# The output projection's sum over the heads by ScalarE and an accumulating DMA

## The chip, the cores and the metric

The kernel runs on one core of one Trainium2 chip. The metric is the device time of one execution in microseconds (us), as the median of several executions. Engines: TensorE (PE), VectorE (DVE), ScalarE (ACT), GpSimd (POOL), and SyncE (SP), which issues the transfers of the kernel before.

## The reference, cut to what matters

Two layers: a Hyena long convolution, then differential attention with 16 heads. 512 positions and 16 meta tokens, width 1024, inner width 2048, all float32. The change lies in the last line of the second layer, the product with `w_out`:

```python
def diff_attention_mixer(h, w_in, lam_vecs, subln, w_out, cos, sin, layer_idx):
    u = h @ w_in                                  # q, k, v, z
    ...
    o = rmsnorm(o, subln, DA_NORM_EPS) * (1.0 - lam_init)      # per head, 128 wide
    return (o.reshape(B, T, D_INNER) * jax.nn.silu(z)) @ w_out
# reference: h = h + rmsnorm(y, norm_post[i]); return h[:, N_META:]
```

The kernel sums this product over the heads: each head gives 128 of the 2048 rows of `w_out`, and `acc` (in SBUF, 4 blocks of 128 positions by 1024 columns) holds the sum.

## The kernel before, in words

Each float32 matmul is made of three products of rounded parts (`hi`, L209, on ACT; `lo`, L212, the rest, on DVE or POOL). The attention stage runs from 855 us to the end. `attend` (L1282) takes one head per step: for four blocks of 128 queries it does `scores` (L1302: matmuls L1315 and L1318 into two `a` tiles of PSUM, maximum L1321 on DVE, exponentials L1322 on ACT into `pp` and `E`, their difference L1326 on DVE, a copy of 80 columns L1327 on POOL), and for the head before it `turn` (L1330: transposes into a `b` tile, casts to `ph`, `pl`) and `weigh` (L1347: the product with the values). Between these, `run` lets a `Filler` put in steps from a list `seq`, by a credit in us: projections of queries and keys of the next head, in odd steps the `z` projections of two heads (L345 into a `b` tile, L1231 on DVE empties it, L1233 is its tanh), in even steps the values of two heads, and the output projection of the head two before. A scheduler then orders the instructions of each engine; the order is fixed in the program. The four `b` tiles ("b", one PSUM bank each) are taken in turn by projections, transposes and products, so that each matmul into a `b` tile waits until the instruction that emptied the same bank four tiles before is done.

The output projection is `o_item` (L1236): for each block `tt` of 128 positions, six matmuls L1249 into two banks, one per half of the 1024 columns. How the banks get into the sum depends on the head. Head 0: ACT writes them (L1262). Heads 1 to 12: DVE multiplies by the row's factor `r` and adds to `acc` (L1264, 128x512, two per block). Head 13: ACT moves both banks to `vl` (L1254) and POOL adds (L1255). Heads 14 and 15: DVE, both banks in one instruction (L1257). Head h's projection stands in step h + 2, so that of head 13 lies beside the last head's weighted sums, in the tail, from some 1387 us on. After the last head, `finish` (L1059 on) applies the norm and writes the output.

The tile `E` also holds the lambda vectors once, ahead of the heads (L1001). `vl` holds the low parts of the values (rows 0 to 3 are used; L1211 puts the fifth row's low part into `vh`).

Of the kernel before, what the change touches and what calls it, by code (L numbers as in the profile page):

```python
# [10 lines left out]
F32 = mybir.dt.float32  # L11
F32R = mybir.dt.float32r
I32 = mybir.dt.int32
AF = mybir.ActivationFunctionType
ALU = mybir.AluOpType
# [4 lines left out]
P = 128  # L20
T = 528
TH = 264
PARTS = ((0, 272, 68), (272, 528, 128))
META = 16
S = 512
D = 1024
E = 2048
KT = 8
NCH = 8
HEADS = 16  # L30
MR = 6 * META
# [102 lines left out]
def view(t, off, *dims, parts=None):  # L134
    pd = list(t.ap[0])
    if parts is not None:
        pd = [pd[0], parts]
    return bass.AP(tensor=t.tensor, offset=t.offset + off, ap=[pd] + [list(x) for x in dims])
# [54 lines left out]
class Trunk:  # L193
# [777 lines left out]
    def attention(self):  # L971
        tc, nc, I = self.tc, self.nc, self.I
        v, g, s, te = nc.vector, nc.gpsimd, nc.scalar, nc.tensor
        with ExitStack() as cx:
            pool = lambda name, **kw: cx.enter_context(tc.tile_pool(name=name, **kw))
            k1 = pool("k1", bufs=1)
            pc = pool("pc", bufs=2)
# [20 lines left out]
            self.load(sub, I["subln"])  # L998
            v.tensor_scalar(sub, sub, 0.5 * (1.0 - LAM_INIT), None, op0=ALU.mult)

            lv = self.tl(pc, [P, 4, 64], F32, "E", bufs=2)  # L1001
            self.load(lv, bass.AP(tensor=I["lam"].tensor, offset=0, ap=[[0, P], [64, 4], [1, 64]]))
            v.tensor_tensor(lv[:, 0::2], lv[:, 0::2], lv[:, 1::2], op=ALU.mult)
            l2 = self.tl(k1, [P, 2], F32, "l2")
# [178 lines left out]
    def v_item(self, pc, u, st):  # L1183

        def body(wv, j):
            te = self.nc.tensor
            if j == 0:
                st["vh"] = self.tl(pc, [P, 5, 256], F32R, "vh", bufs=2)
                st["vl"] = self.tl(pc, [P, 5, 256], F32R, "vl", bufs=2)
            a, b = KTS[j]  # L1190
            n = P if j < 4 else MR
            ps = self.tl(self.psB, [P, 512], F32, "b")
            for k in range(KT):
                wk = slice((k % 4) * 256, (k % 4) * 256 + 256)
                if j < 4:
                    ops = [(self.xh[:, k, a:b], 0), (self.xh[:, k, a:b], 1), (self.xl[:, k, a:b], 0)]
                else:
                    xm = self.xm[:, k].rearrange("p a b c -> p (a b c)")
                    ops = [(xm, 0), (xm, 1)]
                for q, (x, w) in enumerate(ops):  # L1200
                    te.matmul(ps[:n, :256], x, wv[k // 4][w][:, wk], start=(k == 0 and q == 0),  # L1201
                              stop=(k == KT - 1 and q == len(ops) - 1))
            r = self.rv[:n, j:j + 1]
            vh = st["vh"][:n, j]
            self.nc.scalar.activation(vh, ps[:n, :256], AF.Copy, scale=r)
            if j < 4:
                o, lo = slice(0, n), st["vl"][:n, j]
            else:
                o = slice(64, n)
                lo = st["vh"][o, j]  # L1210
            self.nc.vector.scalar_tensor_tensor(lo, ps[o, :256], r[o], vh[o].bitcast(F32), op0=ALU.mult,  # L1211
                                                op1=ALU.subtract)

        return Item([self.I["w_v"][u, i] for i in (0, 1)], [(2.6 if j < 4 else 1.75, lambda w, j=j: body(w, j)) for j in range(5)])

    def z_item(self, pc, st):
# [19 lines left out]
    def o_item(self, pc, st, then=None):  # L1236

        def body(ws, tt):
            (gh, gl), (wh, wl) = st["g"], ws[0]
            r = st["r"][:, tt:tt + 1]  # L1240
            if st["h"] < HEADS - 3:
                pss = [self.tl(self.psB, [P, 512], F32, "b") for _ in (0, 1)]
            else:
                both = self.tl(self.psA, [P, 2, 512], F32, "a")
                pss = [both[:, 0], both[:, 1]]
            sls = [slice(0, 512), slice(512, D)]
            for q, (a, b) in enumerate(((gh, wh), (gh, wl), (gl, wh))):
                for ps, sl in zip(pss, sls):
                    self.nc.tensor.matmul(ps, a[:, tt * P:(tt + 1) * P], b[:, sl], start=q == 0, stop=q == 2)  # L1249
            if st["h"] >= HEADS - 3:  # L1250
                y = self.yo[:, tt].rearrange("p (h n) -> p h n", h=2)
                if st["h"] == HEADS - 3:
                    t = self.tl(pc, [P, 2, 512], F32, "vl", bufs=2)
                    self.nc.scalar.activation(t, both, AF.Copy, scale=r)  # L1254
                    self.nc.gpsimd.tensor_tensor(y, y, t, op=ALU.add)  # L1255
                else:
                    self.nc.vector.scalar_tensor_tensor(y, both, r, y, op0=ALU.mult, op1=ALU.add)  # L1257
                pss = ()
            for ps, sl in zip(pss, sls):
                y = self.yo[:, tt, sl]  # L1260
                if st["h"] == 0:
                    self.nc.scalar.activation(y, ps, AF.Copy, scale=r)  # L1262
                else:
                    self.nc.vector.scalar_tensor_tensor(y, ps, r, y, op0=ALU.mult, op1=ALU.add)  # L1264
            if then:
                then(tt)

        return Item([self.I["w_out1"][st["h"]]], [(1.3, lambda w, tt=tt: body(w, tt)) for tt in range(4)])

    def attend_last(self, pc, st, sub, fill):  # L1270
# [31 lines left out]
    def scores(self, pc, st, qt, nlam):  # L1302

        v, s, te = self.nc.vector, self.nc.scalar, self.nc.tensor
        r2 = lambda t: t.rearrange("p (h t) -> p h t", h=2)
        s0, pr = st["s0"], st["pr"]
        ks, qs, ql = st["ks"], st["qs"], st["ql"]
        p = self.tl(pc, [P, MR + S], F32, "pp", bufs=8)
        es = [p[:, MR - META:], self.tl(pc, [P, T], F32, "E", bufs=2)]
        sm = self.tl(self.small, [P, 4], F32, "sm")  # L1310
        tq = slice(qt * P, (qt + 1) * P)
        pss = [self.tl(self.psA, [P, 2, 512], F32, "a") for _ in (0, 1)]
        for mp in (0, 1):
            for h in (0, 1):
                te.matmul(pss[mp][:, h, :TH], qs[:, mp, tq], ks[:, mp, h * TH:(h + 1) * TH], start=True, stop=False)  # L1315
        for mp in (0, 1):
            for h in (0, 1):
                te.matmul(pss[mp][:, h, :TH], ql[:, mp, tq], ks[:, mp, h * TH:(h + 1) * TH], start=False, stop=True)  # L1318
        for mp, ps in enumerate(pss):
            mx = self.tl(self.small, [P, 1], F32, "mx")  # L1320
            v.tensor_reduce(mx, ps[:, :, :TH], axis=AX.XY, op=ALU.max, negate=True)  # L1321
            s.activation(r2(es[mp]), ps[:, :, :TH], AF.Exp, bias=mx,  # L1322
                         accum_out=s0[:, qt:qt + 1] if mp == 0 else sm[:, 0:1])
        v.reciprocal(sm[:, 1:2], sm[:, 0:1])
        v.scalar_tensor_tensor(sm[:, 2:3], s0[:, qt:qt + 1], nlam, sm[:, 1:2], op0=ALU.mult, op1=ALU.mult)
        v.scalar_tensor_tensor(es[0], es[1], sm[:, 2:3], es[0], op0=ALU.mult, op1=ALU.add)  # L1326
        self.nc.gpsimd.tensor_copy(view(p, 0, [META, 5], [1, META]), view(p, MR - META, [0, 5], [1, META]))  # L1327
        pr.append(p)
# [79 lines left out]
```

## Time and profile before

| | us |
|---|---|
| median of 3 executions | 1432.77 (1430.24 to 1435.04) |
| the profiled execution, its own time | 1434.51 |
| its span, first to last instruction | 1432.4 |
| PE busy in the span | 1342.4 (94%) |
| DVE busy | 1138.2 (79%) |
| ACT busy | 735.2 (51%) |
| POOL busy | 519.1 (36%) |
| mean granted clock of PE, share of full | 0.972 |

The rows of the profile that follow come from this one execution. "Busy" counts time in which an engine works on an instruction; a matmul of 512 columns starts some 0.23 us after the one before it and ends later, since matmuls overlap. A wait is put down to the instruction that released it last. A DMA's time is that from its issue to its landing.

### The profile page before, as it was taken

The page shows a single profiled execution, that of the slowest core. Times are in us where ns is not written, and L with a number is a line of the kernel's source. Part 1 is how long each engine was busy: PE and PEld are TensorE (multiplying, and loading weights), DVE is VectorE, ACT ScalarE, POOL GpSimd, SP SyncE. Part 2 cuts the span into 40 slices and gives each one's busy share as a digit, 9 for nine tenths or more (in the row PEclk, how much of TensorE's full clock was granted, in tenths as well). Part 3 has the DMA queues.
Part 4 walks back from the last instruction along what each step waited for, and adds up shares of the span by engine and source line. Part 5 has one row for each costly group of instructions (what it writes and reads, how often), then busy time and mean ns, then how long its engine had stood idle before and what let it go on. Part 6 is the DMA issues. An engine that isn't in the chain of part 4 may idle for free. (4 is left out here: it accounts for less than half of the span.)

```text
span 1432.4 us, 24736 instructions
## 1 busy us (share of the span) xinstructions
PE 1342.4 (94%) x9296; PEld 1246.3 (87%) x9296; DVE 1138.2 (79%) x2196; ACT 735.2 (51%) x1400; POOL 519.1 (36%) x543
## 2 busy tenths in 40 slices
PE   5889999999999999999887999999999999999994
PEld 4889889999999999999887888897979879797883
DVE  8789988877777777777678687978879687888888
ACT  5355533443333232324447678666567556667653
POOL 7367634532323232323534233223342323324223
PEclk8899999999999999999988999999999999999998
DMA  6343442232323232323310312212021221212221
GB/s 207 103 146 124 145 153 75 74 119 75 104 74 104 75 103 75 103 74 101 95 62 32 132 45 75 70 42 81 31 88 60 67 67 38 82 45 89 89 67 59
DMA packets 63558, 123.47 MB, mean 86 GB/s; under 512 B 7296, under 2 KB 11648, under 8 KB 63440
## 3 DMA queue, kind: packets, MB, share of 16 engines
q1 hardware_dynamic: 63440, 121.91, 26.2%
q8 instruction: 73, 1.20, 0.3%
q14 instruction: 45, 0.37, 0.1%
HBM read 109.30 MB, written 12.58 MB: 85 GB/s over the span
## 5 line engine op out<-in xcount | busy, mean ns | idle before, releaser
L209 ACT CAST wh<-wr 128x512 fp32r<-128x512 f32 x314 | 182.1, 618 | 253.3 <-PE b L348 70.4
L348 PE MATMUL b<-xh,wh 128*128 128x264 f32 x1024 | 264.9, 291 | 3.8 <-ACT wh L209 1.9
L348 PE MATMUL b<-xl,wh 128*128 128x264 f32 x1024 | 263.5, 289 | 2.6 <-DVE xl L458 2.6
L348 PE MATMUL b<-xh,wl 128*128 128x264 f32 x1024 | 258.5, 288 | 0.6 <-POOL wl L212 0.6
L212 DVE TENSOR_TENSOR wl<-wr,wh 128x512 fp32r<-128x512 f32 x250 | 182.7, 760 | 25.3 <-ACT wh L209 24.1
L348 PEld LDWEIGHTS b<-xh,wh 128*128 128x128 f32 x1024 | 184.0, 193 | 7.6 <-ACT wh L209 2.7
L348 PEld LDWEIGHTS b<-xl,wh 128*128 128x128 f32 x1024 | 183.8, 192 | 4.3 <-DVE xl L458 3.9
L348 PEld LDWEIGHTS b<-xh,wl 128*128 128x128 f32 x1024 | 181.7, 192 | 1.1 <-POOL wl L212 0.9
L212 POOL TENSOR_TENSOR wl<-wr,wh 128x512 fp32r<-128x512 f32 x64 | 97.4, 1538 | 83.8 <-ACT wh L209 83.7
L345 PE MATMUL b<-xh,wh 128*128 128x512 f32 x232 | 94.3, 406 | 4.8 <-DVE acc L1264 4.8
L1321 DVE TENSOR_REDUCE mx<-a 128x1 f32<-128x528 f32 x128 | 87.9, 700 | 7.7 <-PE a L1318 7.2
L345 PE MATMUL b<-xl,wh 128*128 128x512 f32 x232 | 93.6, 403 | 0.0
L345 PE MATMUL b<-xh,wl 128*128 128x512 f32 x232 | 93.0, 401 | 0.0
L1264 DVE SCALAR_TENSOR_TENSOR acc<-b,rh,acc 128x512 f32<-128x512 f32 x96 | 70.8, 743 | 25.9 <-PE b L1249 25.3
L1179 POOL TENSOR_TENSOR ro<-ro,rope 128x528 f32<-128x528 f32 (+1 forms) x32 | 43.1, 1347 | 108.6 <-ACT ro L1168 102.1
L514 POOL TENSOR_SCALAR u<-vecs 128x1 f32<-128x1 f32 x96 | 26.4, 296 | 151.7 <-DVE cv L519 133.5
L1327 POOL COPY pp<-pp 128x80 f32<-128x80 f32 x64 | 16.5, 259 | 166.6 <-DVE pp L1326 120.0
L1201 PE MATMUL b<-wh,xh 128*128 128x256 f32 x256 | 73.9, 289 | 0.4 <-DVE vl L1211 0.4
L1201 PE MATMUL b<-wl,xh 128*128 128x256 f32 x256 | 72.8, 284 | 0.0
L1201 PE MATMUL b<-wh,xl 128*128 128x256 f32 x256 | 72.5, 283 | 0.0
L1315 PE MATMUL a<-ks,qs 128*128 128x264 f32 x256 | 56.2, 302 | 10.0 <-ACT qs L209 6.2
L1315 PEld LDWEIGHTS a<-ks,qs 128*128 128x128 f32 x256 | 46.0, 194 | 21.4 <-ACT qs L209 6.4
(383 smaller groups left out, 4036.7 us busy)
## 6 DMA issues: line engine op xcount, KB each, us to landing
wr<-in_w_in SPq DMA_DIRECT2D x128, 256.0 KB, 2.9
wr<-in_w_out SPq DMA_DIRECT2D x64, 256.0 KB, 2.8
hsp<-ho SPq DMA_DIRECT2D x16, 512.0 KB, 2.7
H<-hsp SPq DMA_DIRECT2D x16, 512.0 KB, 3.9
wr<-in_w_k SPq DMA_DIRECT2D x32, 256.0 KB, 2.8
wr<-in_w_q SPq DMA_DIRECT2D x32, 256.0 KB, 2.7
wr<-in_w_z SPq DMA_DIRECT2D x32, 256.0 KB, 2.7
wr<-in_w_v SPq DMA_DIRECT2D x32, 256.0 KB, 2.6
```

Source lines behind the costliest of these rows:

```text
L209: self.nc.scalar.copy(dst, src)
L212: (eng or self.nc.vector).tensor_tensor(dst, src, hi.bitcast(F32), op=ALU.subtract)
L345: te.matmul(ps, w[:, wk], x[:, k, first:T], start=st, stop=sp)
L348: te.matmul(ps[h], w[:, wk], x[:, k, h * TH:(h + 1) * TH], start=st, stop=sp)
L514: g.tensor_scalar(u[:, e:e + 1], b_in[:, mt:mt + 1], -1.0, None, op0=ALU.mult)
L1179: g.tensor_tensor(y, y, rope[:, 1, n0:n0 + n], op=ALU.mult)
L1201: te.matmul(ps[:n, :256], x, wv[k // 4][w][:, wk], start=(k == 0 and q == 0), stop=(k == KT - 1 and q == len(ops) - 1))
L1264: self.nc.vector.scalar_tensor_tensor(y, ps, r, y, op0=ALU.mult, op1=ALU.add)
L1315: te.matmul(pss[mp][:, h, :TH], qs[:, mp, tq], ks[:, mp, h * TH:(h + 1) * TH], start=True, stop=False)
L1321: v.tensor_reduce(mx, ps[:, :, :TH], axis=AX.XY, op=ALU.max, negate=True)
L1327: self.nc.gpsimd.tensor_copy(view(p, 0, [META, 5], [1, META]), view(p, MR - META, [0, 5], [1, META]))
```

## The change

Heads 14 and 15 keep their form. For the heads 1 to 13 each bank of the output projection is now moved by ACT, times `r`, to a tile `yt` of 128x512 (two buffers), and POOL issues a DMA that reads `yt` and adds it to its half block of `acc`. Head 0 is as before. To make room, `E` has one buffer in place of two, and `vl` four rows in place of five. Lines from L1250 on move up by 6.

```diff
--- before.py
+++ after.py
@@ -998,7 +998,7 @@
             self.load(sub, I["subln"])
             v.tensor_scalar(sub, sub, 0.5 * (1.0 - LAM_INIT), None, op0=ALU.mult)
 
-            lv = self.tl(pc, [P, 4, 64], F32, "E", bufs=2)
+            lv = self.tl(pc, [P, 4, 64], F32, "E", bufs=1)
             self.load(lv, bass.AP(tensor=I["lam"].tensor, offset=0, ap=[[0, P], [64, 4], [1, 64]]))
             v.tensor_tensor(lv[:, 0::2], lv[:, 0::2], lv[:, 1::2], op=ALU.mult)
             l2 = self.tl(k1, [P, 2], F32, "l2")
@@ -1186,7 +1186,7 @@
             te = self.nc.tensor
             if j == 0:
                 st["vh"] = self.tl(pc, [P, 5, 256], F32R, "vh", bufs=2)
-                st["vl"] = self.tl(pc, [P, 5, 256], F32R, "vl", bufs=2)
+                st["vl"] = self.tl(pc, [P, 4, 256], F32R, "vl", bufs=2)
             a, b = KTS[j]
             n = P if j < 4 else MR
             ps = self.tl(self.psB, [P, 512], F32, "b")
@@ -1247,21 +1247,15 @@
             for q, (a, b) in enumerate(((gh, wh), (gh, wl), (gl, wh))):
                 for ps, sl in zip(pss, sls):
                     self.nc.tensor.matmul(ps, a[:, tt * P:(tt + 1) * P], b[:, sl], start=q == 0, stop=q == 2)
-            if st["h"] >= HEADS - 3:
-                y = self.yo[:, tt].rearrange("p (h n) -> p h n", h=2)
-                if st["h"] == HEADS - 3:
-                    t = self.tl(pc, [P, 2, 512], F32, "vl", bufs=2)
-                    self.nc.scalar.activation(t, both, AF.Copy, scale=r)
-                    self.nc.gpsimd.tensor_tensor(y, y, t, op=ALU.add)
-                else:
-                    self.nc.vector.scalar_tensor_tensor(y, both, r, y, op0=ALU.mult, op1=ALU.add)
-                pss = ()
-            for ps, sl in zip(pss, sls):
-                y = self.yo[:, tt, sl]
-                if st["h"] == 0:
-                    self.nc.scalar.activation(y, ps, AF.Copy, scale=r)
-                else:
-                    self.nc.vector.scalar_tensor_tensor(y, ps, r, y, op0=ALU.mult, op1=ALU.add)
+            y = self.yo[:, tt].rearrange("p (h n) -> p h n", h=2)
+            if st["h"] > HEADS - 3:
+                self.nc.vector.scalar_tensor_tensor(y, both, r, y, op0=ALU.mult, op1=ALU.add)
+            else:
+                for i, ps in enumerate(pss):
+                    t = y[:, i] if st["h"] == 0 else self.tl(pc, [P, 512], F32, "yt", bufs=2)
+                    self.nc.scalar.activation(t, ps, AF.Copy, scale=r)
+                    if st["h"]:
+                        self.nc.gpsimd.dma_start(y[:, i], t, accum_op=ALU.add)
             if then:
                 then(tt)
 
@@ -1306,7 +1300,7 @@
         s0, pr = st["s0"], st["pr"]
         ks, qs, ql = st["ks"], st["qs"], st["ql"]
         p = self.tl(pc, [P, MR + S], F32, "pp", bufs=8)
-        es = [p[:, MR - META:], self.tl(pc, [P, T], F32, "E", bufs=2)]
+        es = [p[:, MR - META:], self.tl(pc, [P, T], F32, "E", bufs=1)]
         sm = self.tl(self.small, [P, 4], F32, "sm")
         tq = slice(qt * P, (qt + 1) * P)
         pss = [self.tl(self.psA, [P, 2, 512], F32, "a") for _ in (0, 1)]
```

ScalarE in step 7 (the place called so below is at 1060 us of the trace of before): `wh` and `qs` are casts of weights and of rotated queries, `yt` the new staging tile, `th` the tanh of the z gate, `ph` the cast of transposed weights. Before:

```order
L1322 ACTIVATE E_2181_12656,sm_2182_12657<-a_2184_12659,mx_2186_12671 128x528
L209 CAST wh_2247_12947<-wr_2249_12949 128x512
L209 CAST wh_2247_12947<-wr_2250_12953 128x512
L209 CAST qs_2179_12648<-ro_2177_12638 64x512 x4
L1322 ACTIVATE pp_2201_12733,s0_2139_12448<-a_2204_12736,mx_2206_12746 128x528
L1233 ACTIVATE th_2209_12770<-zg_2208_12768 128x512
L209 CAST ph_2213_12788<-b_2212_12783 96x512
L1322 ACTIVATE E_2202_12734,sm_2203_12735<-a_2205_12737,mx_2207_12749 128x528
L1322 ACTIVATE pp_2239_12899,s0_2235_12889<-a_2242_12902,mx_2244_12912 128x528
```

After:

```order
L1316 ACTIVATE E_2213_12720,sm_2214_12721<-a_2216_12723,mx_2218_12735 128x528
L209 CAST wh_2287_13027<-wr_2289_13029 128x512
L209 CAST wh_2287_13027<-wr_2290_13033 128x512
L209 CAST qs_2211_12712<-ro_2209_12702 64x512 x4
L1256 ACTIVATE yt_2229_12785<-b_2227_12777,rh_2161_12435 128x512
L1233 ACTIVATE th_2243_12838<-zg_2242_12836 128x512
L1316 ACTIVATE pp_2235_12801,s0_2171_12512<-a_2238_12804,mx_2240_12814 128x528
L1256 ACTIVATE yt_2230_12788<-b_2228_12778,rh_2161_12435 128x512
L1316 ACTIVATE E_2236_12802,sm_2237_12803<-a_2239_12805,mx_2241_12817 128x528
L209 CAST ph_2249_12860<-b_2248_12855 96x512
L1256 ACTIVATE yt_2246_12849<-b_2244_12841,rh_2161_12435 128x512
L1316 ACTIVATE pp_2279_12979,s0_2275_12969<-a_2282_12982,mx_2284_12992 128x528
```

The evictions of head 5's first block (`yt_2229`, `yt_2230`) and of its second (`yt_2246`, `yt_2247`) come in between: the first behind the four casts of `qs`, the second behind the next `pp`.

PE at the same place, with the semaphores that each row waits for: the last part of a block of the output projection, scores, a transpose, and the start of a z projection (L345). Before:

```order
L1249 MATMUL b_2211_12774<-wh_2188_12691,gh_2124_12351 128x512 [waits DVE_49]
...
L1315 MATMUL a_2242_12902<-ks_2157_12550,qs_2179_12648 128x264 [waits Activation_49]
...
L1318 MATMUL a_2242_12902<-ks_2157_12550,qlo0_1476_9112 128x264 [waits DVE_49]
...
L1336 MATMUL b_2212_12783<-ident_1_66,pp_2046_11948 96x128 [waits DVE_49]
...
L345 MATMUL b_2214_12794<-xh_6_81,wh_2197_12723 128x512 [waits DVE_49]
```

After:

```order
L1249 MATMUL b_2245_12842<-wh_2220_12755,gh_2152_12407 128x512 [waits Activation_49]
...
L1309 MATMUL a_2282_12982<-ks_2189_12614,qs_2211_12712 128x264 [waits Activation_49]
...
L1312 MATMUL a_2282_12982<-ks_2189_12614,qlo0_1476_9112 128x264 [waits DVE_49]
...
L1330 MATMUL b_2248_12855<-ident_1_66,pp_2070_11996 96x128 [waits Activation_49]
...
L1309 MATMUL a_2283_12983<-ks_2189_12614,qs_2211_12712 128x264 [waits Activation_49]
...
L1312 MATMUL a_2283_12983<-ks_2189_12614,qlo0_1476_9112 128x264 [waits DVE_49]
...
L345 MATMUL b_2250_12866<-xh_6_81,wh_2231_12791 128x512 [waits Activation_49]
```

The second bank of the block, the transpose and the z projection waited for DVE and wait for ACT now; one more set of scores (`a_2283`) stands ahead of the z projection.

ScalarE in the tail, at the output projection of head 13; `gh` is the cast of the gated output of head 14. Before:

```order
L1254 ACTIVATE vl_2979_16502<-a_2978_16495,rh_2903_16179 128x1024
L1367 ACTIVATE th_2962_16443<-b_2932_16334 128x512
L209 CAST gh_2963_16446<-zg_2810_15727 128x512
L1254 ACTIVATE vl_2989_16535<-a_2988_16528,rh_2903_16179 128x1024
L209 CAST ph_2973_16482<-b_2972_16477 128x512
L209 CAST ph_2976_16491<-b_2975_16486 128x512
L209 CAST ph_2986_16524<-b_2985_16519 128x512
L1254 ACTIVATE vl_2994_16557<-a_2993_16550,rh_2903_16179 128x1024
L209 CAST ph_2991_16546<-b_2990_16541 128x512
L209 CAST ph_2996_16568<-b_2995_16563 96x512
```

After:

```order
L1256 ACTIVATE yt_3075_16694<-a_3074_16687,rh_2997_16367 128x512
L1256 ACTIVATE yt_3076_16697<-a_3074_16687,rh_2997_16367 128x512
L1361 ACTIVATE th_3058_16635<-b_3028_16526 128x512
L1256 ACTIVATE yt_3086_16730<-a_3085_16723,rh_2997_16367 128x512
L209 CAST gh_3059_16638<-zg_2896_15899 128x512
L1256 ACTIVATE yt_3087_16733<-a_3085_16723,rh_2997_16367 128x512
L209 CAST ph_3069_16674<-b_3068_16669 128x512
L209 CAST ph_3072_16683<-b_3071_16678 128x512
L1256 ACTIVATE yt_3092_16755<-a_3091_16748,rh_2997_16367 128x512
L209 CAST ph_3083_16719<-b_3082_16714 128x512
L209 CAST ph_3089_16744<-b_3088_16739 128x512
L1256 ACTIVATE yt_3093_16758<-a_3091_16748,rh_2997_16367 128x512
```

Four evictions of both banks have become eight of one bank each, two of them with tiles free and six behind a DMA that empties theirs; the casts `ph` stand between them.

## Rows read from the trace of the kernel before

**Rows 1.** The page, first part: busy time, share of the span, instructions

```profile
PE 1342.4 (94%) x9296; PEld 1246.3 (87%) x9296; DVE 1138.2 (79%) x2196; ACT 735.2 (51%) x1400; POOL 519.1 (36%) x543
```

**Rows 2.** Windows, attention stage: busy us (instructions) by engine, PEclk, DMA share, GB/s

```profile
855.00:1387.00 532.00, 515.74 (x3172) 455.26 (x3171) 434.03 (x863) 344.53 (x685) 162.94 (x162) 0.98 0.20 65
```

**Rows 3.** Waits of PE, 855 to 1387 us: us in total, times, longest

```profile
PE b L1249 <- DVE zg L1231: 7.8, 5, 1.6
PE b L345 <- DVE acc L1264: 4.8, 5, 1.6
PE b L1249 <- DVE acc L1264: 1.3, 4, 0.4
```

**Rows 4.** Windows of 20 us that hold a pinch, columns as before

```profile
1060.00:1080.00 20.00, 17.27 (x81) 13.94 (x79) 15.29 (x26) 9.35 (x22) 3.66 (x5) 0.83 0.18 63
...
1140.00:1160.00 20.00, 17.43 (x70) 13.31 (x69) 13.83 (x26) 11.06 (x23) 7.42 (x8) 0.83 0.18 56
1220.00:1240.00 20.00, 17.65 (x78) 13.49 (x78) 15.88 (x27) 13.58 (x27) 8.43 (x8) 0.91 0.33 106
```

**Rows 5.** Timeline of PE at one pinch: start, us, instruction, idle before

```profile
1063.83 0.50 PE L1249 MATMUL b<-wh,gh 128*128 128x512 f32 x1 [1.56 <-DVE zg L1231]
...
1067.38 0.80 PE L345 MATMUL b<-xh,wh 128*128 128x512 f32 x1 [0.82 <-DVE acc L1264]
```

**Rows 6.** Groups by line: instructions; ns min/median/max, first and last start

```profile
L1264 DVE SCALAR_TENSOR_TENSOR acc<-b,rh,acc x96: 719/745/754, 895.6 to 1374.0; 128x512 f32<-128x512 f32 x96
...
L1262 ACT ACTIVATE acc<-b,rh x8: 682/688/713, 857.2 to 875.2; 128x512 f32<-128x512 f32 x8
```

**Rows 7.** Timeline of DVE in the tail, beside POOL's add

```profile
1393.97 2.32 DVE L220 TENSOR_SCALAR rs_a<-vv 128x4 f32<-128x4 f32 x1
```

**Rows 8.** Timeline of POOL in the tail

```profile
1393.88 2.39 POOL L1255 TENSOR_TENSOR acc<-acc,vl 128x1024 f32<-128x1024 f32 x1
```

**Rows 9.** Timeline of PE in the tail

```profile
1397.75 0.50 PE L1360 MATMUL b<-pl,vh 128*128 128x512 f32 x1 [1.73 <-DVE pl L212]
...
1401.58 0.50 PE L1360 MATMUL b<-pl,vh 128*128 128x512 f32 x1 [1.29 <-DVE pl L212]
```

**Rows 10.** Timeline of ACT in the tail

```profile
1388.88 1.11 ACT L1254 ACTIVATE vl<-a,rh 128x1024 f32<-128x1024 f32 x1
...
1400.09 0.58 ACT L209 CAST ph<-b 96x512 fp32r<-96x512 f32 x1 [0.31 <-PE b L1336]
```

**Rows 11.** Timeline of ACT at the same pinch

```profile
1059.34 0.70 ACT L1322 ACTIVATE E<-a,mx 128x528 f32<-128x528 f32 x1 [1.37 <-DVE mx L1321]
...
1061.07 2.53 ACT L209 CAST qs<-ro 64x512 fp32r<-64x512 f32 x4
...
1067.14 0.70 ACT L1322 ACTIVATE E<-a,mx 128x528 f32<-128x528 f32 x1
```

**Rows 12.** Timeline of DVE at the same pinch

```profile
1060.50 0.75 DVE L1264 SCALAR_TENSOR_TENSOR acc<-b,rh,acc 128x512 f32<-128x512 f32 x1
1061.17 1.40 DVE L1326 SCALAR_TENSOR_TENSOR pp<-E,sm,pp 128x528 f32<-128x528 f32 x1
...
1063.10 0.68 DVE L1231 TENSOR_TENSOR zg<-b,rb 128x512 f32<-128x512 f32 x1
```

**Rows 13.** DMA by name: issues, KB each, median us from issue to landing

```profile
H<-hsp SPq DMA_DIRECT2D x16, 512.0 KB, 3.9
...
xt<-in_xT SPq DMA_DIRECT2D x8, 264.0 KB, 5.6
...
out<-acc SPq DMA_DIRECT2D x8, 256.0 KB, 2.0
...
ks<-h1d SPq DMA_DIRECT2D x2, 512.0 KB, 5.0
```

**Rows 14.** Timeline of DVE between the pinches

```profile
1015.46 0.74 DVE L1264 SCALAR_TENSOR_TENSOR acc<-b,rh,acc 128x512 f32<-128x512 f32 x1
...
1020.97 0.75 DVE L1264 SCALAR_TENSOR_TENSOR acc<-b,rh,acc 128x512 f32<-128x512 f32 x1
```

## The prediction

> **What bounds the kernel now.** I read the page's engine line first, then the windows by stage, then who waits for whom in the attention stage, then 20-us windows there, and last one place instruction by instruction. TensorE (PE) is busy for 94% of the span [rows 1]. In the attention stage, 855 to 1387 us, it is busy for 515.7 of 532 us; VectorE (DVE) has 434.0, ScalarE (ACT) 344.5, GpSimd (POOL) 162.9 [rows 2]. So the most that any change to the other engines can give back there is the 16.3 us in which PE stands, and what its clock loses because of them. The waits of PE say where those lie: 7.8 us are waits of the output projection for `zg` (L1231 on DVE), 4.8 us waits of a z projection (L345) and 1.3 us waits of the output projection for the evictions L1264 [rows 3]; all are waits for a PSUM bank that DVE has to empty. The two large ones stand five times each, and the five fall together at one place per two heads, which I call the pinch. Of its 20-us windows three have a granted clock under 1 [rows 4]: 0.83, 0.83 and 0.91, where half clock (1.2 GHz) for 6.8, 6.8 and 3.6 us would make these means; at half clock half of the work is lost, so 3.4 + 3.4 + 1.8 = 8.6 us. PE had just stood for 1.56 us when the clock fell [rows 5], at 1063.83. The top of any gain is thus 7.8 + 4.8 + 1.3 + 8.6, about 22 us.
>
> **What is removed.** 96 DVE evictions of 0.745 us [rows 6], 71.5 us of DVE. In the windows where PE doesn't wait this is worth nothing: PE is full there, and DVE gets idle time. At the pinch it is worth something only if DVE still ends last. At the tail POOL's four adds and ScalarE's four evictions of head 13 go; beside one such add a DVE operation on 128x4 took 2.32 us [rows 7, 8], and PE then waited 1.73 and 1.29 us for `pl` of DVE [rows 9]. Worth up to 3.0 us.
>
> **What is added on ScalarE.** 104 evictions into `yt`. The nearest row is head 0's eviction of the same shape, 0.688 us [rows 6]: 71.6 us, less head 13's four of 1.11 [rows 10] = 67 us. ACT goes from 344.5 to some 410 of 532 us, so as a sum it fits. In place it doesn't: the order shows that at the pinch the new eviction `yt_2229` stands behind the four casts of `qs`, which end at 1061.07 + 2.53 = 1063.60 [rows 11], and that the second bank of the projection's next block (`b_2245`), which waited for DVE, now waits for it. That eviction ends at 1063.60 + 0.69 = 1064.3. Before, the same bank's matmuls began at 1063.83 [rows 5]. So DVE's wait is replaced by one for ACT of the same length or 0.5 us more; the relief of DVE (the eviction at 1060.50 ahead of L1326 and L1231 [rows 12]) is not on the path any more.
>
> **What is added by two staging tiles.** `yt` has two buffers, so the third eviction waits until the first one's DMA has landed. I call C the time from the end of an eviction to that landing: POOL's issue, the transfer, and the add. At the pinch `yt_2246` is the third one, and the z projection `b_2250` waits for it: it can start at 1064.3 + C + 0.69 = 1065.0 + C. Before, it started at 1067.38 [rows 5], and in the new order one more set of scores (four matmuls; by [rows 1] some 4 x 1342.4 / 9296 = 0.6 us) stands ahead of it, so that 1068.0 costs nothing. The pinch grows by C - 3.0 us, and not below zero, as ACT has `E` at 1067.14 to do first [rows 11].
>
> **C is not in this trace**: no DMA is issued from POOL and none adds. The nearest rows are transfers of SyncE (SP) [rows 13]: 256 KB out of the very tile `acc` land after 2.0 us, which is the low end. An add has to read both operands, so I look at 512 KB: 3.9 and 5.0 us. The high end is 5.6 us, the slowest load of about 256 KB. I take C = 4.5, the middle of the 512 KB rows, the nearest to what has to move. The pinch then costs 1.5 us, five times: **+7.7 us**; by the ends 0 and 13.2. The half-clock spells I leave as they are, since a pause of the same length stays.
>
> The Trainium skill, "DMA: Bandwidth & Descriptors", section "Anatomy of one DMA — SWDGE (gpsimd) path", gives a DMA issued by GpSimd about 2.0 us plus its bytes at 436 KB per us; by that, an estimate, 256 KB take 2.6 us, the pinch costs nothing, and the whole comes out at the third rival below. The section doesn't price an add, and no run so far shows one.
>
> **Heads between the pinches.** There the first evictions of two projections are 5.5 us apart (1015.46 and 1020.97 [rows 14]); two buffers turn round in C + 0.69 = 5.2 us. It fits, by 0.3 us. Above C = 4.8 it doesn't, and what is over shows on PE once the banks' slack is used.
>
> **The tail.** Head 13's evictions stand on ACT between the casts `ph` that the last heads' weighted sums need. Before, the last of these casts began at 1400.09 and ended at 1400.67 [rows 10]. After, by the order: the first `yt` ends at 1388.88 + 0.69 = 1389.57, its DMA lands C later, then follow eviction, cast `gh` (0.6) and eviction up to 1391.55 + C; another C until this one's tile is free, an eviction and the cast: 1392.8 + 2C. With C = 4.5 that is 1401.8, **+1.1 us**. The 3.0 us that DVE gets back don't show, as PE then waits for the casts. With 5.6: +3.3; with 2.0: nothing, and -3.0 counts in full.
>
> **Edits at nothing.** `E` with one buffer: its exponentials are issued at 1059.34 and 1067.14, and L1326, which reads it, ends at 1061.17 + 1.40 [rows 11, 12]; without that distance one exponential, 0.70 us, would wait per quarter. Row 4 of `vl`, unused, costs nothing. POOL issues 104 DMAs: even at 1.3 us of POOL each, 135 on top of 162.9 fit into 532 [rows 2]. Queued behind them on POOL are the 80-column copies L1327, `gl` and the rotations; the copies are needed a whole quarter later, `gl` can be late by the wait for its `yt`. SP's queue carries the same instructions, and the added bytes (104 x 256 KB, read twice and written) go in a stage where the DMA engines are busy for 0.20 of the time [rows 2].
>
> **The sum.** 1434.5 (the profiled execution; its span is 1432.4) + 7.7 + 1.1 = 1443.3. It stands 1.7 over the median of the runs shown, so **1441.6, say 1442 us**, 0.6% slower. With C = 2.0: 1434.5 - 3.0 - 1.7 = 1430. With C = 5.6: 1434.5 + 13.2 + 3.3 - 1.7 = 1449, and up to 5 us more where two buffers are too few between the pinches: 1454.
>
> **Rivals.**
> First, *long DMAs*: C = 7 or more, because the add runs at a fraction of a copy's rate or POOL is slow to issue. Then the pinch costs 4.0 us five times (20), the tail 6.1, and six heads between the pinches fall behind by (7.7 - 5.5) + (7.7 - 6.3) = 3.6 us each, of which about 2 lie under free banks: 10 us. 1434.5 + 36 - 1.7 = 1469. For it: nothing in the trace bounds the add. Against: no landing of 256 KB is above 5.6.
> Second, the other side, *DVE's relief counts*: the mechanism is the bank wait for L1231 at the pinch. At 1060.50 DVE does an eviction ahead of L1326, the maximum and L1231. Without it L1231 ends 0.75 us earlier, and L1326, which took 1.40 beside a POOL operation, ends earlier too. If ACT's eviction slips in before the casts of `qs` (they wait for `ro`, not for PE) or the casts run shorter, PE's wait of 1.56 goes with it, five times 1.5, and with a pause under half a microsecond the clock doesn't fall: 7.8 + 8.6 = 16 us. 1434.5 - 16.4 - 1.7 = 1416. It decides from an ACT that reaches `yt_2229` before 1062.7. Against: the order on ACT is fixed, and the casts stand ahead.
> Third, *nothing to be measured*: C of 2 to 3 us; the pinch keeps its length, the tail gives up to 3 us. 1430 to 1433.
>
> **How the numbers follow.** About 0.3% (4.3 us) is what a measurement of this kernel can tell from no change: 1428.5 to 1437.1. Forecast 0.48 (C of 3.5 to 5.6, 1437 to 1454), long DMAs 0.14, relief of DVE 0.18, nothing 0.20. Faster 0.20, same 0.22, slower 0.58. Range: 1420 to 1470, which leaves out the larger part of the relief and DMAs of over 7 us, some 2 in 10.
>
> **What would show it.** In the trace after: ACT's new evictions near 0.69 us; PE at the pinches waiting for ACT, not for L1231; the z projection behind `yt_2246` about C + 1 us after `yt_2229` ended; DVE near 363 of 532 us in the attention stage. The DMA rows give C: it is the number that I am least sure of. The forecast is wrong if C is under 3.2 or over 6, or if PE's waits at the pinch are gone.

## The result, and the profile after

The changed kernel takes 1442.83 us (median of 5 executions, 1437.85 to 1450.23), the kernel before 1430.24 in the same comparison (1428.43 to 1435.04): a ratio of 1.009, 95% interval 1.0067 to 1.0113. In the comparisons of the experiments below the kernel before has medians of 1431.5 to 1432.3 (13 to 21 executions), so the change costs 10 to 13 us. The profiled execution takes 1441.26 us, its span 1439.5 against 1432.4.

The page of the changed kernel: engines, the queue of the new DMAs, the group of their issues on POOL, and their time to landing.

```profile
PE 1343.7 (93%) x9296; PEld 1245.9 (87%) x9296; DVE 1090.2 (76%) x2100; ACT 789.0 (55%) x1500; POOL 595.9 (41%) x643
...
q0 software_dynamic: 14976, 27.27, 11.2%
...
L1258 POOL DMA_DIRECT2D acc<-yt x104 | 90.5, 899 | 147.1 <-ACT yt L1256 144.1
...
acc<-yt POOLq DMA_DIRECT2D x104, 256.0 KB, 3.7
```

The DMA with the add costs POOL 0.90 us of issue each, and lands after 3.7 us (median). The windows of the attention stage and of its pinches that lost clock (columns as in [rows 2]):

```profile
855.00:1387.00 532.00, 508.47 (x3130) 447.17 (x3129) 381.01 (x756) 392.44 (x770) 244.77 (x258) 0.99 0.48 111
1060.00:1080.00 20.00, 16.30 (x70) 12.41 (x69) 13.83 (x23) 12.19 (x26) 9.29 (x11) 0.91 0.43 92
1240.00:1260.00 20.00, 18.80 (x107) 16.56 (x108) 9.15 (x27) 10.01 (x20) 6.99 (x9) 0.91 0.52 103
1320.00:1340.00 20.00, 16.28 (x80) 13.05 (x81) 11.56 (x21) 11.13 (x23) 9.23 (x11) 0.91 0.54 117
```

DVE went from 434.0 us [rows 2] to 381.0, ACT from 344.5 to 392.4, POOL from 162.9 to 244.8. PE has 508.5 where it had 515.7. Three windows have a clock of 0.91, where two had 0.83 and one 0.91 [rows 4]. Waits of PE, 855 to 1387 us (us in total, times, longest), and then those of ACT for the DMAs:

```profile
PE b L345 <- ACT yt L1256: 9.5, 5, 2.0
PE b L1249 <- ACT yt L1256: 4.9, 6, 0.9
PE a L1309 <- ACT E L1316: 3.7, 6, 1.0
...
PE a L1309 <- ACT pp L1316: 1.2, 5, 0.2
...
PE b L1249 <- DVE zg L1231: 0.3, 1, 0.3
```

```profile
ACT yt L1256 <- DMA acc<-yt: 32.4, 24, 3.4
```

The waits for `zg` and for L1264 [rows 3] have become waits for `yt`, again five times at a z projection and five times (and once more near 898 us) at an output projection, and six for `E`. One pinch, in the timelines of PE, ACT and POOL (start, us, instruction, idle before):

```profile
1065.55 0.50 PE L1249 MATMUL b<-wh,gh 128*128 128x512 f32 x1 [0.90 <-ACT yt L1256]
...
1068.51 0.51 PE L1309 MATMUL a<-ks,qs 128*128 128x264 f32 x2 [0.54 <-ACT E L1316]
...
1071.13 0.80 PE L345 MATMUL b<-xh,wh 128*128 128x512 f32 x1 [1.87 <-ACT yt L1256]
```

```profile
1062.25 2.54 ACT L209 CAST qs<-ro 64x512 fp32r<-64x512 f32 x4 [0.59 <-POOL ro L1180]
1064.81 0.69 ACT L1256 ACTIVATE yt<-b,rh 128x512 f32<-128x512 f32 x1
...
1070.39 0.69 ACT L1256 ACTIVATE yt<-b,rh 128x512 f32<-128x512 f32 x1 [1.47 <-DMA acc<-yt]
```

```profile
1063.31 2.97 POOL L212 TENSOR_TENSOR wl<-wr,wh 128x512 fp32r<-128x512 f32 x2
1066.23 0.86 POOL L1258 DMA_DIRECT2D acc<-yt  x1
```

The first eviction ends at 1064.81 + 0.69 = 1065.50. POOL is still at `wl` and issues its DMA at 1066.23; the third eviction, on the same tile, starts at 1070.39, 4.9 us after the first ended, and the z projection begins at 1071.13, when that eviction is done. This is the chain that the prediction laid out, 1.87 us of idle PE against 0.82 before [rows 5].

In the tail ACT waits for the DMAs, first at the last evictions of head 12 and then, at those of head 13, between the casts:

```profile
1377.12 0.69 ACT L1256 ACTIVATE yt<-b,rh 128x512 f32<-128x512 f32 x1 [3.40 <-DMA acc<-yt]
...
1382.47 0.69 ACT L1256 ACTIVATE yt<-b,rh 128x512 f32<-128x512 f32 x1 [2.35 <-DMA acc<-yt]
...
1396.66 1.27 ACT L1256 ACTIVATE yt<-a,rh 128x512 f32<-128x512 f32 x2 [0.59 <-PE a L1249]
...
1405.72 0.69 ACT L1256 ACTIVATE yt<-a,rh 128x512 f32<-128x512 f32 x1 [1.47 <-DMA acc<-yt]
...
1408.35 0.57 ACT L209 CAST ph<-b 96x512 fp32r<-96x512 f32 x1
```

The last cast `ph` ends at 1408.35 + 0.57 = 1408.92, where it ended at 1400.67 before [rows 10]. The norm of head 13 (`vv`) on DVE and PE's last matmuls, first before the change and then after it:

```profile
1369.07 0.15 DVE L1385 TENSOR_TENSOR vv<-b,i 128x4 f32<-128x4 f32 x1
...
1416.65 0.62 PE L1249 MATMUL a<-wh,gl 128*128 128x512 f32 x2
```

```profile
1374.00 0.16 DVE L1379 TENSOR_TENSOR vv<-b,i 128x4 f32<-128x4 f32 x1 [0.53 <-PE b L1375]
...
1423.48 0.63 PE L1249 MATMUL a<-wh,gl 128*128 128x512 f32 x2
```

The stage had come in 4.9 us late by `vv`, and PE's last matmuls begin 6.8 us late, so the tail added 1.9. It adds them ahead of head 13's evictions: from `vv` to the first of these it is 1396.66 - 1374.00 = 22.7 us, where it was 1388.88 [rows 10] - 1369.07 = 19.8 (+2.85). PE stands for 3.0 us in this stretch (1.85 for `zg`, 0.80 for `pp`, 0.33 for `vl`), where it had no wait; ahead of these stand casts of weights, which ACT does only after its two waits for the DMAs. From there to PE's last matmuls it is 26.8 us, where it was 27.8 (-0.95).

### The profile page after: what moved, and what is told of

Same layout as the page of the kernel before. It is cut to its first block, busy times and chain, and to the rows that moved or that the text cites. A ratio compares the mean times of both kernels' runs of the same rounds, so it can differ in the third digit from the quotient of the medians.

```text
span 1439.5 us, 25017 instructions
## 1 busy us (share of the span) xinstructions
PE 1343.7 (93%) x9296; PEld 1245.9 (87%) x9296; DVE 1090.2 (76%) x2100; ACT 789.0 (55%) x1500; POOL 595.9 (41%) x643
## 3 DMA queue, kind: packets, MB, share of 16 engines
q0 software_dynamic: 14976, 27.27, 11.2%
## 5 line engine op out<-in xcount | busy, mean ns | idle before, releaser
L212 DVE TENSOR_TENSOR wl<-wr,wh 128x512 fp32r<-128x512 f32 x250 | 197.1, 818 | 45.2 <-ACT wh L209 43.3
L1258 POOL DMA_DIRECT2D acc<-yt x104 | 90.5, 899 | 147.1 <-ACT yt L1256 144.1
L212 POOL TENSOR_TENSOR wl<-wr,wh 128x512 fp32r<-128x512 f32 x64 | 92.9, 1520 | 51.5 <-ACT wh L209 51.4
L345 PE MATMUL b<-xh,wh 128*128 128x512 f32 x232 | 95.5, 412 | 10.8 <-ACT yt L1256 9.5
L345 PE MATMUL b<-xh,wl 128*128 128x512 f32 x232 | 93.5, 403 | 0.0
L345 PE MATMUL b<-xl,wh 128*128 128x512 f32 x232 | 93.3, 402 | 0.0
L1256 ACT ACTIVATE yt<-b,rh 128x512 f32<-128x512 f32 x96 | 65.1, 689 | 41.6 <-DMA acc<-yt 32.4
```

Of the source, the lines that this page charges most:

```text
L212: (eng or self.nc.vector).tensor_tensor(dst, src, hi.bitcast(F32), op=ALU.subtract)
L345: te.matmul(ps, w[:, wk], x[:, k, first:T], start=st, stop=sp)
L1256: self.nc.scalar.activation(t, ps, AF.Copy, scale=r)
L1258: self.nc.gpsimd.dma_start(y[:, i], t, accum_op=ALU.add)
```

## The experiments

Theory A: the loss is the wait for a staging tile until its DMA has landed. Theory B: it is ScalarE's place and load. Theory C: it is `E` with one buffer. All ratios are to the kernel before, with 95% intervals; runs of 5 rounds unless said.

**Four staging tiles.**

```diff
-... self.tl(pc, [P, 512], F32, "yt", bufs=2)
+... self.tl(pc, [P, 512], F32, "yt", bufs=4)
-        gh = self.tl(pc, [P, S], F32R, "gh", bufs=3)        # gl alike
+        gh = self.tl(pc, [P, S], F32R, "gh", bufs=2)
```

> Four staging tiles in place of two; the space comes from the tiles of the gated output (gh, gl: two buffers in place of three, which leaves the order of all instructions as it is). Theory A, the loss is the wait for a staging tile until its DMA has landed: the z projections' wait for yt (9.5 us in the attention stage after the change, five times 1.8 to 2.0) falls under 2 us, the evictions' wait for DMAs (32.4 us on ScalarE) under 5, and the time to 1433 to 1437 us. Theory B, the loss is ScalarE's place and load (the new evictions behind the casts of qs): the waits move but their sum stays near 24 us, and the time at 1440 to 1445. Theory C, the loss is E with one buffer: as B.

1421.47 us, 0.9918 (0.9902 to 0.9934). Waits of PE in the attention stage, and the stage's window:

```profile
PE b L1249 <- ACT yt L1256: 5.3, 6, 0.9
PE a L1309 <- ACT pp L1316: 2.1, 6, 0.9
```

```profile
855.00:1387.00 532.00, 520.05 (x3231) 458.05 (x3229) 397.42 (x793) 406.67 (x797) 255.89 (x268) 1.00 0.49 116
```

The z projection no longer waits for `yt` at all (9.5 us before this edit), ACT waits for no DMA, and the clock is 1.00 over the stage. So A, but with 21 us where it said 6 to 10: the clock also stays full, and the scheduler, which sees no wait for tiles, orders the pinch otherwise (the extra set of scores goes behind the z projection). This run alone doesn't separate the tiles from that order; the next two come closer to it. What is left, 0.9 us per pinch, is the first eviction behind the casts of `qs`: B's place exists and is the smaller part in this order.

**An addition on POOL in place of the DMA**, two tiles as in the change.

```diff
-                        self.nc.gpsimd.dma_start(y[:, i], t, accum_op=ALU.add)
+                        self.nc.gpsimd.tensor_tensor(y[:, i], y[:, i], t, op=ALU.add)
```

> The changed kernel with the DMA replaced by an addition on POOL (tensor_tensor on 128x512), still with two staging tiles. ScalarE's order at the pinch stays but for one eviction that comes a place earlier. Theory A: a tile is free about 1.4 to 2 us after its eviction, as in the copies L1180 of the same size (1.30 us), against 4.9 us at the pinch after the change; the z projection's wait for yt goes (9.5 us to under 2) and the time to 1424 to 1432 us, though POOL is busy 104 x 1.3 = 135 us longer. Theory B: the waits for yt stay, 1438 us or more.

1426.87 us, 0.9970 (0.9956 to 0.9984). Waits of PE, and the group of the additions:

```profile
PE b L1249 <- ACT yt L1256: 5.4, 6, 0.9
...
PE b L1249 <- DVE zg L1231: 2.2, 4, 1.0
```

```profile
L1258 POOL TENSOR_TENSOR acc<-acc,yt x104: 1256/1292/1759, 901.9 to 1400.0; 128x512 f32<-128x512 f32 x104
```

With an addition of 1.29 us in place of a DMA that lands after 3.7 two tiles do: the z projection doesn't wait for `yt`, while the waits at the casts of `qs` (5.4 us) are as after the change (4.9). (L1180, which the expectation calls a copy, is an addition of this size.) This speaks for A most directly, since ScalarE's order at the pinch is the changed kernel's but for one place: same tiles, same evictions, 16 us less. A part of the 16 is the clock, 1.00 over the stage against 0.99.

**The DMA without the add** (this leaves the sum over the heads out), all orders as after the change.

```diff
-                        self.nc.gpsimd.dma_start(y[:, i], t, accum_op=ALU.add)
+                        self.nc.gpsimd.dma_start(y[:, i], t)
```

> The same DMAs as plain copies, without the add (the sum over the heads is left out); the order of all instructions is the same as after the change. If the add has a price of its own, the time to landing falls from 3.7 us to about 2.8 and, by theory A, each of the five pinches is shorter by as much: 1437 to 1439 us. If the add is free: 3.5 to 3.7 us and 1441 to 1444 us. Theories B and C: 1441 to 1444 either way.

1435.85 us, 1.0021 (1.0007 to 1.0034). Issues and landing; the third eviction and the z projection at the pinch:

```profile
L1258 POOL DMA_DIRECT2D acc<-yt x104 | 56.7, 545 | 157.7 <-ACT yt L1256 149.1
...
acc<-yt POOLq DMA_DIRECT2D x104, 256.0 KB, 2.3
```

```profile
1068.08 0.69 ACT L1256 ACTIVATE yt<-b,rh 128x512 f32<-128x512 f32 x1
...
1073.14 0.69 ACT L1256 ACTIVATE yt<-b,rh 128x512 f32<-128x512 f32 x1 [0.95 <-DMA acc<-yt]
```

```profile
1073.88 0.50 PE L345 MATMUL b<-xh,wh 128*128 128x512 f32 x1 [1.36 <-ACT yt L1256]
```

The add costs 1.4 us of landing (2.3 against 3.7) and 0.35 of issue (0.545 against 0.899), and 7 us of the whole, more than the 4 to 6 expected. At this pinch the time from eviction to free tile is 1073.14 - 1068.77 = 4.37 us against 4.89, and PE's wait 1.36 against 1.87: 0.5 each, one for one, as A says. It is less than 1.4 because this one DMA lands after 3.6 us here and 4.1 after the change, both above the medians; the wait for POOL's `wl` is the same 0.7. But little of this reaches the whole stage: over the five pinches the z projection's wait falls from 9.5 to 7.6 us, and the wait for `zg` rises from 0.3 to 2.1.

The larger part of the 7 us lies in the tail: from `vv` of head 13 (1376.88) to PE's last matmuls (1421.92) it is 45.0 us against 49.5. Of these 4.4 us 3.4 come ahead of head 13's first eviction (1396.18), since ACT no longer waits for DMAs at the last evictions of head 12. So with the same order of all instructions those two waits, 3.40 and 2.35 us, are what made the tail long after the change, more than head 13's own evictions.

**One staging tile** (3 rounds).

```diff
-... self.tl(pc, [P, 512], F32, "yt", bufs=2)
+... self.tl(pc, [P, 512], F32, "yt", bufs=1)
```

> One staging tile in place of two, so that every eviction waits for the DMA of the one before. Theory A, with some 4.2 us from an eviction's end to the landing: at each pinch the second and the third eviction wait in a row and the z projection starts about 5 us later, 25 us; between the pinches eight evictions take 8 x 4.9 = 39 of a head's 42.6 us and come in pairs, some 5 us per head, 30 us; the tail 15 to 20 us. 1500 to 1525 us. If the time is not bound by these tiles (theory B), under 1460.

1556.1 us, 1.0869 (1.0842 to 1.0895), 113 us over the changed kernel, more than A's 57 to 82. ACT's waits and the window of the stage:

```profile
ACT yt L1256 <- DMA acc<-yt: 91.0, 43, 4.9
```

```profile
855.00:1387.00 532.00, 464.99 (x2666) 397.47 (x2664) 323.69 (x631) 334.61 (x652) 210.55 (x220) 0.93 0.39 91
```

PE has 465.0 of 532 us and a clock of 0.93. The miss is that I counted stops at the staging tile alone. The clock fell too (0.99 after the change), and PE's wait for `E` rose from 3.7 to 10.0 us, as the exponentials stand behind the evictions on ACT. How the 31 us above the bound divide isn't shown.

**E in two buffers again, within the change** (space from `gh`, `gl`; the order of every engine stays).

```diff
-        es = [..., self.tl(pc, [P, T], F32, "E", bufs=1)]
+        es = [..., self.tl(pc, [P, T], F32, "E", bufs=2)]
```

> The changed kernel with E in two buffers again (the space comes from gh and gl); the order of all instructions is the same as after the change. It asks whether the one buffer of E costs anything by itself. Theory A, and the prediction's term of nothing for it: within 3 us of the changed kernel, 1440 to 1446 us, PE's wait for E (3.7 us in the attention stage after the change) as it is. Theory C: PE's wait for E goes, 1436 to 1439 us.

1443.42 us, 1.0085 (1.0068 to 1.0102). Waits of PE:

```profile
PE b L345 <- ACT yt L1256: 9.3, 5, 2.0
PE b L1249 <- ACT yt L1256: 5.4, 6, 0.9
PE a L1309 <- ACT E L1316: 3.7, 6, 1.0
```

Nothing moves: the wait for `E` is 3.7 us with either, so it is the exponential's place on ACT, not its tile. Theory C falls.

**The smaller tiles alone, in the kernel before.**

```diff
-        es = [..., self.tl(pc, [P, T], F32, "E", bufs=2)]
+        es = [..., self.tl(pc, [P, T], F32, "E", bufs=1)]
-                st["vl"] = self.tl(pc, [P, 5, 256], F32R, "vl", bufs=2)
+                st["vl"] = self.tl(pc, [P, 4, 256], F32R, "vl", bufs=2)
```

> The kernel before with only the two smaller tiles: E with one buffer, vl with four rows. Theory A: no more than 2 us from the kernel before, 1429 to 1433 us. Theory C: E with one buffer makes a good part of the 12 us, 1435 to 1442 us, and PE waits for E or for scores in the attention stage.

1424.63 us, 0.9948 (0.9931 to 0.9965): faster, which no theory said. Waits of PE:

```profile
PE b L1249 <- DVE zg L1231: 8.5, 5, 1.9
```

The z projection's 4.8 us for L1264 [rows 3] are gone, and the clock is 1.00 over the stage against 0.98. `vl` alone leaves every order as it was; `E` alone gives exactly this kernel's orders: with one buffer the scheduler puts the casts of `qs` ahead of those of `wh`, and, at the pinch, two sets of scores between the output projection and the z projection, where one stood. So 8 us lie in the order of the kernel before; the tile as such costs nothing. Against this kernel the change costs 18 us (1442.8 against 1424.6).

**The new form at the odd heads alone** (those at the pinch), two tiles; and **at the even heads alone** (and head 13).

```diff
+                    if st["h"] and not (st["h"] % 2):       # even: % 2 == 0 or h == 13
+                        self.nc.vector.scalar_tensor_tensor(y[:, i], ps, r, y[:, i], op0=ALU.mult, op1=ALU.add)
+                        continue
```

> The new form with two staging tiles at the odd heads alone, those whose projection stands at the pinch (and head 13); the even heads keep DVE's eviction. On ScalarE the casts of qs come ahead of the casts of wh at the pinch, other than after the change. Theory A: the waits for yt at the pinch stay, the time within 4 us of the changed kernel, 1438 to 1446 us. Theory B (the place behind the casts is what counts): 1428 to 1434 us, as the first eviction comes a microsecond earlier.

> The complement: the new form with two staging tiles at the even heads and head 13, DVE's eviction at the pinches; there ScalarE's order is that of the kernel before (casts of wh, then of qs). Theory A: the pinch is as in the kernel before (waits of the output projection for zg and of the z projection for L1264), two tiles suffice between the pinches, and the time is 1429 to 1434 us. If two tiles are too few between the pinches too: 1437 us or more, with waits of PE for yt there.

Odd: 1439.09 us, 1.0052 (1.0032 to 1.0073). Even: 1438.49, 1.0050 (1.0031 to 1.0068). Waits of PE, first odd, then even:

```profile
PE b L1249 <- ACT yt L1259: 3.9, 6, 0.9
PE b L1333 <- ACT yt L1259: 3.3, 5, 0.7
...
PE b L345 <- ACT yt L1259: 0.9, 3, 0.3
```

```profile
PE b L1333 <- DVE acc L1256: 8.9, 6, 1.8
PE b L345 <- DVE acc L1256: 5.6, 5, 1.1
```

Odd agrees with A in time and rules out B's 1428 to 1434; but with the casts of `qs` first, the waits for `yt` sit at the transposes and the output projection (7.2 us) and hardly at the z projection (0.9), so it tells less of the place than I had hoped. Even: at the pinch PE waits for DVE again, though at the transposes and the z projection and hardly at the output projection; ACT waits for DMAs for 1.4 us only, so two tiles do suffice between the pinches, as A says; yet the time is 4 us over its bound. In the profiled execution 2.7 us of the loss come from `vv` of head 13 on (PE's last matmul at 1420.23, `vv` at 1369.91), all of it ahead of head 13's first eviction (1392.52), and 2.4 ahead of the attention stage, which the edit doesn't touch (first `vv` at 839.50 against 837.07); the rest stays open.

**The odd heads with four tiles** (space from `gh`, `gl`).

> The new form with four staging tiles at the odd heads alone (at the pinches) and at head 13; the even heads keep DVE's eviction. ScalarE casts qs before wh here. Theory A: as with four tiles everywhere, since the new form between the pinches brings nothing on PE's path: 1419 to 1426 us. If four tiles everywhere are better because DVE is relieved between the pinches: 1428 us or more.

1430.03 us, 0.9987 (0.9977 to 0.9998): a miss for A. PE and ACT at a pinch:

```profile
1063.98 0.50 PE L1249 MATMUL b<-wh,gh 128*128 128x512 f32 x1 [2.23 <-ACT yt L1259]
```

```profile
1060.69 2.53 ACT L209 CAST qs<-ro 64x512 fp32r<-64x512 f32 x4 [1.95 <-POOL ro L1180]
1063.24 0.69 ACT L1259 ACTIVATE yt<-b,rh 128x512 f32<-128x512 f32 x1
```

No wait for a tile is left, but PE stands 2.23 us for the first eviction, which stands behind the casts of `qs`, which wait for POOL's `ro`. In this order these waits come to 12.6 us, six in all, 7.3 more than with four tiles everywhere (5.3), of the 8.6 us between the two kernels; DVE's relief between the pinches, which the expectation would name, isn't needed for it. So the number of tiles decides only once ScalarE gets to the eviction in time.

**Three tiles and E in two buffers** (space from `gh`, `gl`).

> Three staging tiles and E in two buffers. At the pinch the third eviction is the one that the z projection waits for, so by theory A three tiles are enough there: PE's wait for yt at the z projection goes, ScalarE still waits for some DMAs, 1421 to 1428 us. If it takes four tiles: 1432 us or more.

1420.54 us, 0.9912 (0.9893 to 0.9931). Waits of PE at z projections are gone, ACT waits 8.0 us for DMAs, and 5.4 us stay at the casts of `qs`. Three tiles do, as A says of the third eviction; the time is level with that of four tiles (the intervals overlap), and below both kernels of the comparison.

**Head 13 in its old form.**

```diff
+            if st["h"] == HEADS - 3:
+                t = self.tl(pc, [P, 2, 512], F32, "vl", bufs=2)
+                self.nc.scalar.activation(t, both, AF.Copy, scale=r)
+                self.nc.gpsimd.tensor_tensor(y, y, t, op=ALU.add)
```

> The changed kernel with head 13 in its old form (both banks to vl by ScalarE, the add on POOL). By the prediction's term for the tail (1.1 us) and by the traces (1.9 us) the time falls by 1 to 2 us: 1440 to 1442 us; PE waits twice for pl beside POOL's adds again, some 3 us. If the tail is the larger part of the loss, it falls by 4 us or more, under 1439.

1448.07 us, 1.0107 (1.0090 to 1.0124): a median 5 us above the changed kernel's in place of 1 to 2 below, though the two intervals overlap. From `vv` of head 13 to PE's last matmul it takes 1.5 us longer than after the change: from head 13's first eviction on (1400.14 to 1428.79) 28.7 us against 26.8, while ACT's waits at head 12's last evictions ahead of it stay (3.38 and 2.05 us). So head 13's new form isn't a loss against POOL's adds in this order, and the expectation had put the 1.9 us at the wrong head. The rest lies ahead of the tail: `vv` of head 13 comes at 1377.82 against 1374.00. The kernel with E in two buffers, of the changed kernel's very order, has it at 1377.41, so some 3 us there are scatter between executions, and I put nothing down to the edit but the 1.5.

## Why the prediction was right, point by point

The forecast was 1442 us, 0.6% slower; measured 1442.8, 0.9%. The sum stood on 1432.8 us for the kernel before, which has 1430.2 in this comparison, so +9 us was forecast and 10 to 13 came. The mechanism holds, but that the two numbers agree to 1 us is in good part luck, as the terms show.

**The pinch.** Its steps stand as they were laid out: the eviction behind the casts of `qs`, the wait of PE that changes from DVE to ACT, the z projection behind the third eviction. C was taken as 4.5 us; it is 4.9 at the pinch shown, 0.7 until POOL has done `wl` and 4.1 to the landing (3.7 is the median of all). The waits of PE at these places, 7.8 + 4.8 + 1.3 = 13.9 us [rows 3], became 9.5 + 4.9 + 3.7 + 1.2 + 0.3 = 19.6: +5.7, and +6.7 in the other kernel of the same order shown above (9.3 + 5.4 + 3.7, with 1.2 and 1.0 for `pp` and `zg`), where the forecast had +7.7 (five times its 1.5 is 7.5). Inside this sum three terms differ and offset each other. The z projection's waits rose by 4.7, not 7.7: one pinch stood for five, and its wait of 0.82 us before isn't that of the others (0.18 to 1.60). The output projection's fell from 9.1 to 5.2, where the forecast had them stay or grow by 0.5 each. The waits for scores behind `E` and `pp`, counted as none, came to 4.9.

**The clock** was to stay as it was, as pauses of the same length stay. There are 3 spells of 3.6 us at half clock in place of 6.8 + 6.8 + 3.6, so 3.2 us less were lost, but the length of the pause doesn't tell which pinch has one. After the 1.87 us before 1071.13 the clock fell; at the next pinch it did not (1.00 in the windows from 1140 to 1180 us):

```profile
1157.21 0.50 PE L345 MATMUL b<-xh,wh 128*128 128x512 f32 x1 [1.89 <-ACT yt L1256]
```

The kernel with E in two buffers, of the same order, has four spells. So I can't put the 3.2 down to the change. (The second rival took it that a pause under half a microsecond keeps the clock: in the attention stage before there are eight, of 0.18 to 0.37 us, and the clock fell at none.)

**The tail**: +1.1 forecast, +1.9 measured, but not where it was forecast. Two times C do follow each other at head 13's evictions, yet from the first of them on the tail is 0.95 us shorter, as PE's waits for `pl` beside POOL's adds [rows 9] are gone, a gain that the forecast didn't count. The loss of 2.85 us lies ahead of them, where ACT waits for the DMAs of head 12, which the forecast left out.

These three terms make 5.7 - 3.2 + 1.9 = 4.4 of the span's 7.1 us. The attention stage began 0.8 us earlier (the first `vv` at 836.30 against 837.07). Of the other 3.5 us 1.0 is in PE's remaining waits in the stage (2.6 against 1.6 us, those for L1211 on DVE above all); 2.5 I can't put down to a row. Part is that each of PE's stops makes the first matmul after it longer (0.50 against 0.39), and there are more stops.

**E with one buffer** was costed at nothing. In the changed kernel that is right (same order, same time). As an edit of the kernel before it is worth 8 us by the order that it brings about, which no trace of before could show; the diff's three edits don't add up.

**POOL** was allowed 1.3 us per issue; it took 0.90. **DVE** was to fall to 363 us and stands at 381 in a window that holds less of the work; its operations were longer, as in the last section.

**Rivals.** The relief of DVE (1416) didn't come, for the reason given: ScalarE isn't there in time (PE still stands 0.90 us for the first eviction at the pinch shown). Where tiles suffice the time does come to 1420.5 to 1421.5, but most of that isn't DVE's relief: with all of DVE's evictions kept and only the smaller tiles it is 1424.6, so the new form with enough tiles is some 3 us better than that, hardly more than the intervals can tell. The long DMAs (1469) didn't come, with C at 4.9 and not 7. No change to be measured needed a C of 2 to 3 us; the DMA without the add, landing after 2.3, comes near to that with 1.0021, and the add takes it away. The Trainium skill ("DMA: Bandwidth & Descriptors", "Anatomy of one DMA — SWDGE (gpsimd) path") gives 2.6 us by its fit, an estimate near the plain copy's 2.3; it doesn't price the add, with which the DMA lands after 3.7.

## What to carry to other kernels

When a producer hands its tile to a DMA, count how many tiles it needs until the first is free again: eviction to landing, the issuing engine's queue included, against the distance of the producer's uses at the tightest place. Two tiles lost 10 to 13 us here, three, with another order at the pinch, gained 12, and with an addition of 1.3 us in place of the DMA two were enough. And before crediting an edit, make its side edits alone: here a smaller tile by itself, through the order that it led to, gained 8 us, nearly as much as the whole change lost.

## What the runs showed that I had not expected

An accumulating DMA of 256 KB from SBUF to SBUF occupies POOL for 0.86 us (median) and lands after 3.7 us; a plain copy of the same bytes 0.54 and 2.3. The queue moved 14976 packets in the one case, 8320 in the other: 144 and 80 per DMA.

POOL's issues stand in order behind its arithmetic: at the pinch the first waits 0.7 us for `wl`. And two of DVE's operations were slow beside that arithmetic. DVE at the pinch of the changed kernel:

```profile
1060.87 1.37 DVE L1319 SCALAR_TENSOR_TENSOR sm<-s,nlam,sm 128x1 f32<-128x1 f32 x1
...
1064.17 2.66 DVE L212 TENSOR_TENSOR qlo<-ro,qs 64x512 fp32r<-64x512 f32 x2
```

The first has one element per partition and takes 0.21 to 0.22 us elsewhere (1057.05, 1069.08); it runs beside POOL's addition L1180 and ends with it (1060.91 + 1.31 = 1062.22). The second, two operations, took 0.72 + 0.69 us before (1063.70, 1065.12) and runs beside POOL's `wl`. DVE was relieved of 71 us of evictions, and its busy time in the stage's window fell by 53 only. Its splits `wl` take 0.925 us each there against 0.778 before (77 and 80 of them), its `qlo` 0.949 against 0.730 (26 each), together 17 us; that POOL's work beside them is the cause throughout is argued from the two lines, not shown.
